# RWKV stage of a hybrid encoder: two PSUM banks for the outputs, one for x, scores of a and r in banks of their own, first retention step one round later

## The chip, the cores and the metric

The kernel runs on one core of a Trainium2 chip. The metric is the device time of one launch in microseconds: the median of three runs before the change is 3579.34 us, from 3575.51 to 3581.64.

## The reference, cut to what matters

Two layers, each with a mixer of three head groups (retention, RWKV-7, differential attention) and a feed-forward part, over 1024 positions of 1024 features in float32. The change touches the RWKV-7 group and the retention group that is recorded beside it. The recurrence that the RWKV stage computes, for six heads of 64 and two directions, is

```
def step(S, inp):
    w_t, k_t, v_t, r_t, a_t, b_t = inp
    S = (S * w_t[..., None, :]
         + jnp.einsum('dbhvk,dbhk->dbhv', S, a_t)[..., None] * b_t[..., None, :]
         + v_t[..., :, None] * k_t[..., None, :])
    return S, jnp.einsum('dbhvk,dbhk->dbhv', S, r_t)
_, ys = lax.scan(step, jnp.zeros((2, B, H, N, N), f32), seqs)
y = ys[0] + jnp.flip(ys[1], 1)
```

Retention is `scores @ V` with a decay mask inside chunks of 128, and a state per chunk that a scan carries on.

## The kernel before, in words

The scan over 1024 steps is done in chunks of 64: inside a chunk the steps are solved with a 64 by 64 triangular inverse, between chunks a state S is handed on. Two heads share the 128 partitions, so there are three head pairs; with two directions and two halves of the sequence that makes twelve units a layer, and each unit has eight chunks.

For a unit, `rwkv_prep` (L514) loads its inputs, forms decays (a scan, tile `cs`, L547) and exponentials, and then the tiles `AR` (a and r side by side), `B` and `K`. Then it multiplies `B` with `AR` on TensorE: in the kernel before, four chunks at a time, a and r together, into a PSUM tile `sbp` of one bank. VectorE masks the r half into `BP` and ScalarE copies the a half into `N` in four pieces. `rwkv_inv` inverts the 32 by 32 blocks of `N` on VectorE (tiles `NB`, `YB`, `TB`), `rwkv_merge` (L639) joins them (`z3ps`, `y3ps`, `zps`, `yps`; L674 is a transpose on VectorE), `rwkv_key` makes `SK` and `kT`, and `rwkv_prod` makes `P`.

The chain itself is `rwkv_rec` (L731), one chunk a call in four steps: `x` on TensorE, `U` (a copy of x by ScalarE), `ns` on TensorE, and `S` (ScalarE) with the output `y` (TensorE). `rwkv` (L856) runs rounds w = -2 to 11 of 16 slots each. In a round the chain handles the second half of unit w and the first half of unit w + 1, interleaved two slots apart; beside it, generators get a number of steps per round: the preparation of unit w + 4 has 13, the inverse of w + 3 has 16, key and merge of w + 2 have 6 and 12, and retention (`ret_all`) has `RSTEP` = 10. Round -2 has no chain step yet. The outputs of a round collect in one PSUM tile `y`; in slot 2 of the following round ScalarE (first half of the sequence) or VectorE (second half) reads it.

After the loop every instruction of an engine is tied to the one recorded before it, so the order on each engine inside the stage is the order of recording. Only against instructions outside the stage, the projections ahead of it, may the scheduler still shift it.

PSUM has eight banks here: two pools of two for all passing tiles (`bank`, L959, takes them in turn), and four for `x` (two), `ns` (one) and `y` (one).

Of the kernel before, what the change touches and what calls it, by code (L numbers as in the profile page):

```python
# [10 lines left out]
F32 = mybir.dt.float32  # L11
F32R = mybir.dt.float32r
AF = mybir.ActivationFunctionType
ALU = mybir.AluOpType
# [155 lines left out]
def _ori(ap, d, off, n):  # L170
    return ap[:, off:off + n] if d == 0 else _rev(ap, off, n)


def _ch(ap, t=64):
    return ap.rearrange("p (c t) -> p c t", t=t)


class Net:
# [335 lines left out]
    def rwkv_prep(self, l, st, u, d, res):  # L514

        nc, X = self.nc, self.X
        p = st["p"]
        dd = self.der[l][:, 18 + p * 8:18 + (p + 1) * 8]
        o = (u if d == 0 else 1 - u) * 512
        lo = []  # L520
        for s in range(2):
            t = X.tile([128, 512], F32, tag=f"lo{s}", name="lo")
            nc.sync.dma_start(out=t, in_=self.lod[s][:, o:o + 512])
            lo.append(t)
        ld = []
        for i, src in enumerate((self.kkd, self.xrd, self.xkd)):
            t = X.tile([128, 512], F32, tag=f"q{i}", name=("kkh", "xrh", "xkh")[i], bufs=1)
            nc.sync.dma_start(out=t, in_=src[p][:, o:o + 512])
            ld.append(t)
        yield 1  # L530
        ps = self.bank([128, 512], "wps")
        self.mm(ps, self.l2[:, d, 0], lo[0])
        yield
        lw = X.tile([128, 512], F32, tag="t1", name="lw")
        self.act(lw, ps, AF.Tanh, scale=0.5, bias=dd[:, d:d + 1])
        self.free(ps)
        ps = self.bank([128, 512], "aps")
        self.mm(ps, self.l2[:, d, 1], lo[1])
        yield
        cf = CF  # L540
        self.act(lw, lw, AF.Identity, scale=cf, bias=self.cf[:, 0:1])
        ta = X.tile([128, 512], F32, tag="t4", name="ta")
        self.act(ta, ps, AF.Tanh, scale=0.5, bias=dd[:, 2 + d:3 + d])
        self.free(ps)
        yield
        e2 = cs = X.tile([128, 512], F32, tag="t2", name="cs")
        nc.vector.tensor_tensor_scan(cs, self.c[:, K_RST:K_RST + 512], _ori(lw, d, 0, 512), 0.0,  # L547
                                     ALU.mult, ALU.add)
        e1 = self.e1
        yield  # L550
        self.act(e1[:, :, 1:65], _ch(cs), AF.Exp)
        self.act(cs, cs, AF.Exp, scale=-1.0)
        wc = X.tile([128, 8], F32, tag="WC", name="WC", bufs=5)

        kd = X.tile([128, 512], F32, tag="t1", name="kd")
        self.act(kd, ta, AF.Identity, scale=dd[:, 4:5], bias=dd[:, 5:6])
        yield
        self.act(wc, e1[:, :, 64])
        ar = X.tile([128, 8, 2, 64], F32, tag="AR", name="AR", bufs=5)

        BP = X.tile([128, 8, 128], F32, tag="BP", name="BP", bufs=3)
        B = X.tile([128, 8, 64], F32, tag="B", name="B", bufs=3)
        K = X.tile([128, 8, 64], F32, tag="K", name="K", bufs=3)
        rm = self.c[:, K_RM:K_RM + 128]
        kko = _ch(_ori(ld[0], d, 0, 512))
        xro = _ch(_ori(ld[1], d, 0, 512))
        tao = _ch(_ori(ta, d, 0, 512))
        ke = X.tile([128, 8, 64], F32, tag="t6", name="ke")
        nc.vector.scalar_tensor_tensor(out=ke, in0=kko, scalar=-0.5, in1=_ch(e2), op0=ALU.mult, op1=ALU.mult)
        q = [slice(4 * b, 4 * b + 4) for b in range(2)]  # L570
        self.tt(ar[:, q[0], 1, :], xro[:, q[0]], e1[:, q[0], 1:65], ALU.mult)

        N = X.tile([128, 8, 64], F32, tag="N", name="N", bufs=3)
        for b in range(2):
            yield
            nc.vector.scalar_tensor_tensor(out=B[:, q[b]], in0=tao[:, q[b]], scalar=1.0, in1=ke[:, q[b]],
                                           op0=ALU.add, op1=ALU.mult)
            self.tt(ar[:, q[b], 0, :], kko[:, q[b]], e1[:, q[b], 0:64], ALU.mult)
            if b == 0:
                self.tt(ar[:, q[1], 1, :], xro[:, q[1]], e1[:, q[1], 1:65], ALU.mult)  # L580
        yield 1
        for b in range(2):

            ps = self.bank([128, 4, 128], "sbp")
            for n in range(4):
                self.mm2(ps[:, n], B[:, 4 * b + n], ar[:, 4 * b + n].rearrange("p a t -> p (a t)"))
            if b == 0:
                self.tt(kd, kd, ld[2], ALU.mult)
                kv, ev = (_ch(kd), _ch(e2)) if d == 0 else (_ch(kd)[:, ::-1, :], _ch(e2)[:, :, ::-1])
            else:  # L590
                self.tt(K, kv, ev, ALU.mult)
                nc.sync.dma_start(out=self.kdd[p][d, :, o:o + 512], in_=kd)
            yield
            self.tt(BP[:, q[b], 64:128], ps[:, :, 64:128], rm[:, None, 64:128].to_broadcast([128, 4, 64]),
                    ALU.mult)
            self.act(N[0:32, q[b]], ps[0:32, :, 0:64])
            self.act(N[32:64, q[b], 0:32], ps[32:64, :, 32:64])
            self.act(N[64:96, q[b]], ps[64:96, :, 0:64])
            self.act(N[96:128, q[b], 0:32], ps[96:128, :, 32:64])
            self.free(ps)  # L600
        res.update(N=N, d=d, i=p * 4 + u * 2 + d, AR=ar, BP=BP, WC=wc, B=B, K=K)

    def rwkv_inv(self, a):
# [35 lines left out]
    def rwkv_merge(self, a):  # L639

        nc = self.nc
        N, L, NB, N3 = a["N"], self.L, a["NB"], self.N3[a["i"] % 2]

        Ld, Z, Yd = NB[:, 0:8], NB[:, 8:16], N[:, :, 0:32]
        H4 = [slice(hb * 32, hb * 32 + 32) for hb in range(4)]
        ps = self.bank([128, 8, 32], "z3ps")
        for n in range(8):
            for hb, r in enumerate(H4):
                self.mm(ps[r, n], N3[r, n], Ld[r, n], tile_position=(hb * 32, hb * 32))
        yield  # L650
        self.act(Z, ps)
        self.free(ps)
        yield 1
        ps = self.bank([128, 8, 32], "y3ps")
        for n in range(8):
            for hb, r in enumerate(H4):
                self.mm(ps[r, n], Yd[r, n], Z[r, n], stop=False, tile_position=(hb * 32, hb * 32))
            for hb, r in enumerate(H4):
                self.mm(ps[r, n], self.ident[r, r], Ld[r, n], start=False, tile_position=(hb * 32, hb * 32))
        yield  # L660
        y22, zt = N[:, :, 0:32], N[:, :, 32:64]
        for hb in (1, 3, 0, 2):
            r = H4[hb]
            self.act(L[r, :, hb % 2 * 32:hb % 2 * 32 + 32], ps[r])
        self.free(ps)
        yield 1

        ps = self.bank([128, 512], "zps")
        for n in range(8):
            for h in range(2):  # L670
                r = h * 64
                self.mm(ps[r + 32:r + 64, n * 32:(n + 1) * 32], N[r:r + 32, n, 32:64], L[r:r + 32, n, 0:32],
                        tile_position=(r, r + 32))
        nc.vector.transpose(out=y22, in_=L[:, :, 32:64])  # L674
        yield
        for r in (32, 96):
            self.act(zt[r:r + 32], ps[r:r + 32, 0:256].rearrange("p (n j) -> p n j", j=32))
        self.free(ps)
        yield 1
        ps = self.bank([128, 512], "yps")  # L680
        for n in range(8):
            for r in (32, 96):
                self.mm(ps[r:r + 32, n * 32:(n + 1) * 32], y22[r:r + 32, n, :], zt[r:r + 32, n, :],
                        tile_position=(r, r))
        yield
        for r in (32, 96):
            self.act(L[r:r + 32, :, 0:32], ps[r:r + 32, 0:256].rearrange("p (n j) -> p n j", j=32))
        self.free(ps)
# [42 lines left out]
    def rwkv_rec(self, st, u, d, s, n, y):  # L731

        nc = self.nc
# [3 lines left out]
        V = self.Vd[(2 * st["p"] + nh) % 4][:, c]  # L737
        S = st["S"][d]
        SK, AR, P = s["SK"][:, n], s["AR"][:, n], s["P"][:, n]
        x = self.psr.tile([128, 64], F32, tag="x", name="x", bufs=2)  # L740
        self.mm2(x, SK[:, 0:64], V, stop=S is None)
        if S is not None:
            self.mm2(x, AR[:, 0], S, start=False)
# [112 lines left out]
    def rwkv(self, l):  # L856
# [32 lines left out]
        ret = [self.ret_all(l), RSTEP, 0, 0]  # L889
        first = len(self.nc.cur_bb.bb.instructions)  # L890
        active, outs = [], []
        for w in range(-2, 12):
            p, j = divmod(w, 4)
            beside = []
# [10 lines left out]
            q, j2 = divmod(w + 2, 4)  # L905
# [3 lines left out]
                beside.append([self.rwkv_bonus(l, sts[p]), 12, 0, 0])  # L909
            if w > 0 and j == 0:  # L910
                beside.append([self.rwkv_fin(l, sts[p - 1]), 13, 0, 0])
            beside.append(ret)
            for g in range(16):
                n, k = divmod(g, 4)
                if g == 0 and -2 < w < 12:
                    y = self.psr.tile([128, 2, 4, 64], F32, tag="y", name="y")

                for i, m in ((w, n + 4), (w + 1, n)):
                    if 0 <= i < 12 and w > -2 and k == i % 2 * 2:
# [716 lines left out]
```

## Time and profile before

| what | value |
|---|---|
| median of three runs | 3579.34 us |
| profiled execution | 3579.7 us |
| its span, first to last instruction | 3577.9 us |
| TensorE busy | 3222.8 us, 90% of the span |
| VectorE busy | 2004.6 us, 56% |
| ScalarE busy | 1576.7 us, 44% |
| GpSimd busy | 943.7 us, 26% |
| mean granted TensorE clock | 0.946 |
| rounds -1 to 11 of layer 0 | from about 590 to 965 us |
| rounds -1 to 11 of layer 1 | from about 2358 to 2731 us |

A row of the profile names engine, line, operation, output and inputs by the program's names. PE is TensorE's matmul, PEld its weight load, DVE VectorE, ACT ScalarE, SP the queue that issues most transfers. Since `L194`, `L188` and `L185` are the lines of helpers that record every matmul, tensor-tensor operation and activation, the tile names tell the place. A number in square brackets is idle time of the engine just ahead of the row, and behind the arrow stands what ended it. A float32 matmul of the program stands in the trace as two records.

### The profile page before, as it was taken

The numbers are of one execution on the slowest core, as the hardware profiler recorded it, in microseconds if no ns is written. First come the engines' busy times: TensorE is split into PE (matmuls) and PEld (weight loads), VectorE is DVE, ScalarE is ACT, GpSimd is POOL, SyncE is SP. The second block draws the span as 40 slices with busy tenths as digits, with TensorE's granted clock in tenths as the row PEclk, the third lists the DMA queues.
The fourth block names the chain that finished last, engine by engine and source line by source line (L and its number), as shares of the span: only waits on it lengthen the run. The fifth ranks groups of instructions, "written<-read, shape, count | busy, mean of one in ns | idle before, by whom it ended". The sixth has DMA issues, their size and how long they took to land. (4 is left out here: it accounts for less than half of the span.)

```text
span 3577.9 us, 69843 instructions
## 1 busy us (share of the span) xinstructions
PE 3222.8 (90%) x28380; PEld 2601.8 (73%) x28380; DVE 2004.6 (56%) x3749; ACT 1576.7 (44%) x3071; POOL 943.7 (26%) x800
## 2 busy tenths in 40 slices
PE   6999797898787999999989997978986989999997
PEld 4777586787565888888867775867774758888886
DVE  4698425766329555552338974167662485555523
ACT  4566443666424333342236664346654342333322
POOL 3222120000026544532132221200000364554220
PEclk9999798998888999999989998989988989999998
DMA  5444334432341222283053433244325212223821
GB/s 167 154 147 123 112 106 132 145 124 72 127 146 47 86 80 83 83 285 121 26 161 123 151 117 118 96 143 139 122 83 175 83 59 80 86 83 99 278 71 47
DMA packets 214057, 418.93 MB, mean 117 GB/s; under 512 B 23876, under 2 KB 58948, under 8 KB 213700
## 3 DMA queue, kind: packets, MB, share of 16 engines
q1 hardware_dynamic: 191000, 378.53, 32.2%
q10 hardware_dynamic: 12672, 23.07, 1.7%
q0 software_dynamic: 10064, 12.85, 1.6%
q8 instruction: 224, 3.67, 0.4%
q14 instruction: 97, 0.79, 0.1%
HBM read 313.67 MB, written 100.70 MB: 116 GB/s over the span
## 5 line engine op out<-in xcount | busy, mean ns | idle before, releaser
L188 POOL TENSOR_TENSOR wll<-wr,whh 128x512 fp32r<-128x512 f32 x416 | 558.4, 1345 | 1616.8 <-ACT whh L185 1610.9
L185 ACT ACTIVATE whh<-wr 128x512 fp32r<-128x512 f32 x416 | 261.1, 631 | 625.8 <-PE sp L194 166.0
L194 PE MATMUL dps<-hl,whh 128*128 128x512 f32 x960 | 383.7, 400 | 6.6 <-DVE hl L188 3.6
L194 PE MATMUL dps<-hh,whh 128*128 128x512 f32 x960 | 387.7, 404 | 1.1 <-DVE stl L377 1.0
L194 PE MATMUL dps<-hh,wll 128*128 128x512 f32 x960 | 383.1, 399 | 0.4 <-POOL wll L188 0.4
L194 PE MATMUL sp<-hh,whh 128*128 128x512 f32 x704 | 279.2, 397 | 9.2 <-ACT hh L185 8.6
L194 PE MATMUL sp<-hl,whh 128*128 128x512 f32 x704 | 281.8, 400 | 2.1 <-POOL hl L188 1.9
L194 PE MATMUL sp<-hh,wll 128*128 128x512 f32 x704 | 276.9, 393 | 1.3 <-POOL wll L188 1.3
L194 PE MATMUL dn<-hl,whh 128*128 128x512 f32 x704 | 274.9, 391 | 0.5 <-DVE hl L188 0.5
L194 PE MATMUL dn<-hh,whh 128*128 128x512 f32 x704 | 274.1, 389 | 1.3 <-ACT hh L185 1.3
L194 PE MATMUL dn<-hh,wll 128*128 128x512 f32 x704 | 273.9, 389 | 0.0
L188 POOL TENSOR_TENSOR wll<-ws,whh 128x512 fp32r<-128x512 f32 x132 | 194.1, 1470 | 177.2 <-ACT whh L185 177.2
L188 DVE TENSOR_TENSOR hl<-hidr,hh 128x512 fp32r<-128x512 f32 x144 | 138.2, 977 | 170.4 <-ACT hh L185 161.5
L194 PEld LDWEIGHTS dps<-hl,whh 128*128 128x128 f32 x960 | 183.6, 191 | 51.8 <-POOL hl L188 6.1
L194 PE MATMUL sp<-sl,whh 128*128 128x512 f32 x528 | 211.3, 400 | 8.8 <-POOL sl L188 6.1
L194 PEld LDWEIGHTS dps<-hh,whh 128*128 128x128 f32 x960 | 183.7, 191 | 45.9 <-issue 4.4
L194 PE MATMUL sp<-sh,whh 128*128 128x512 f32 x528 | 209.8, 397 | 3.1 <-ACT as L185 3.1
L194 PEld LDWEIGHTS dps<-hh,wll 128*128 128x128 f32 x960 | 183.2, 191 | 38.8 <-issue 2.4
L194 PE MATMUL sp<-sh,wll 128*128 128x512 f32 x528 | 211.0, 400 | 0.0
L185 ACT ACTIVATE whh<-ws 128x512 fp32r<-128x512 f32 x132 | 83.5, 632 | 242.7 <-PE sp L194 138.5
L185 ACT ACTIVATE pt<-pt,mx 128x1024 f32<-128x1024 f32 x128 | 147.0, 1149 | 59.6 <-DVE mx L1216 57.3
L194 PEld LDWEIGHTS sp<-hh,whh 128*128 128x128 f32 x704 | 133.9, 190 | 41.1 <-ACT hh L185 9.4
(275 smaller groups left out, 7297.6 us busy)
## 6 DMA issues: line engine op xcount, KB each, us to landing
hidr<-hid SPq DMA_DIRECT2D x144, 256.0 KB, 4.9
bias<-t SPq DMA_DIRECT2D x64, 512.0 KB, 3.8
wr<-in_w_in_dram SPq DMA_DIRECT2D x120, 256.0 KB, 2.9
wr<-in_w_gate_dram SPq DMA_DIRECT2D x44, 512.0 KB, 3.4
wr<-in_w_up_dram SPq DMA_DIRECT2D x44, 512.0 KB, 3.3
wr<-in_w_down_dram SPq DMA_DIRECT2D x44, 512.0 KB, 4.1
pr<-st SPq DMA_DIRECT2D x56, 256.0 KB, 2.3
lo<-lod SPq DMA_DIRECT2D x48, 256.0 KB, 3.2
```

Of the source, the lines that this page charges most:

```text
L185: self.nc.scalar.activation(out=out, in_=in_, func=func, **kw)
L188: (eng or self.nc.vector).tensor_tensor(out=out, in0=a, in1=b, op=op)
L194: self.nc.tensor.matmul(out, lhsT, rhs, start=start, stop=stop, **kw)
```

## The change

Five edits. In `rwkv_prep` the scores of a and of r become two products of eight chunks each, in a bank of their own: `sap`, read by ScalarE alone, and `srp`, read by VectorE alone, one step later; `K` is formed between them. In `rwkv_merge` the transpose of L674 is recorded one step later. `x` has one PSUM buffer, `y` two. In round -2 retention gets one step, its first loads, recorded ahead of the slots, and no other.

```
-        for b in range(2):
-            ps = self.bank([128, 4, 128], "sbp")
-            for n in range(4):
-                self.mm2(ps[:, n], B[:, 4 * b + n], ar[:, 4 * b + n].rearrange("p a t -> p (a t)"))
...
-            yield
-            self.tt(BP[:, q[b], 64:128], ps[:, :, 64:128], rm[:, None, 64:128].to_broadcast([128, 4, 64]),
-                    ALU.mult)
-            self.act(N[0:32, q[b]], ps[0:32, :, 0:64])
...
+        ps = self.bank([128, 8, 64], "sap")
+        for n in range(8):
+            self.mm2(ps[:, n], B[:, n], ar[:, n, 0])
+        self.tt(kd, kd, ld[2], ALU.mult)
...
+        yield
+        self.act(N[0:32], ps[0:32])
+        self.act(N[64:96], ps[64:96])
+        self.act(N[32:64, :, 0:32], ps[32:64, :, 32:64])
+        self.act(N[96:128, :, 0:32], ps[96:128, :, 32:64])
+        self.free(ps)
+        self.tt(K, kv, ev, ALU.mult)
+        nc.sync.dma_start(out=self.kdd[p][d, :, o:o + 512], in_=kd)
+        yield 1
+        ps = self.bank([128, 8, 64], "srp")
+        for n in range(8):
+            self.mm2(ps[:, n], B[:, n], ar[:, n, 1])
+        yield
+        self.tt(BP[:, :, 64:128], ps, rm[:, None, 64:128].to_broadcast([128, 8, 64]), ALU.mult)
+        self.free(ps)
...
-        nc.vector.transpose(out=y22, in_=L[:, :, 32:64])
         yield
         for r in (32, 96):
             self.act(zt[r:r + 32], ps[r:r + 32, 0:256].rearrange("p (n j) -> p n j", j=32))
         self.free(ps)
+        nc.vector.transpose(out=y22, in_=L[:, :, 32:64])
...
-        x = self.psr.tile([128, 64], F32, tag="x", name="x", bufs=2)
+        x = self.psr.tile([128, 64], F32, tag="x", name="x", bufs=1)
...
-            beside.append(ret)
+            if w > -2:
+                beside.append(ret)
+            else:
+                next(ret[0])
...
-                    y = self.psr.tile([128, 2, 4, 64], F32, tag="y", name="y")
+                    y = self.psr.tile([128, 2, 4, 64], F32, tag="y", name="y", bufs=2)
```

VectorE at the end of the projections, before: `st` ends the projections, `rsw` and `rq` are retention's rotation, and `cs` (L547), `ke`, `AR` and `B` belong to the preparation of unit 2 in round -2.

```order
L389 SCALAR_TENSOR_TENSOR st<-st,dps 128x512 x2
L188 TENSOR_TENSOR rsw<-rsw,rope 128x1024
L188 TENSOR_TENSOR rq<-rq,rope 128x1024
L547 SCALAR_TENSOR_TENSOR cs<-c,lw 128x512
L188 TENSOR_TENSOR rq<-rq,rsw 128x1024
L569 SCALAR_TENSOR_TENSOR ke<-kkh,cs 128x512
L188 TENSOR_TENSOR AR<-xrh,e_3467 128x4x64
L188 TENSOR_TENSOR SK<-skp,c 128x512
```

The same place in the changed kernel, where `xs` is the last but one step of the projections:

```order
L407 SCALAR_TENSOR_TENSOR xs<-raw,par_74,xs 128x511
L389 SCALAR_TENSOR_TENSOR st<-st,dps 128x512 x2
L569 SCALAR_TENSOR_TENSOR ke<-kkh,cs 128x512
L188 TENSOR_TENSOR AR<-xrh,e_3467 128x4x64
L188 TENSOR_TENSOR SK<-skp,c 128x512
L576 SCALAR_TENSOR_TENSOR B<-ta,ke 128x256
L188 TENSOR_TENSOR AR<-kkh,e_3467 128x4x64
```

The three retention rows are gone from here, and so is the scan of `cs`. It now stands some thirty rows earlier, ahead of the projections' steps of the second head pair (`xs`, L405):

```order
L638 STREAM_TRANSPOSE N<-NB 128x8x32
L547 SCALAR_TENSOR_TENSOR cs<-c,lw 128x512
L405 SCALAR_TENSOR_TENSOR xs<-raw,par_74,xs 128x511
L407 SCALAR_TENSOR_TENSOR xs<-raw,par_74,xs 128x512
L405 SCALAR_TENSOR_TENSOR xs<-raw,par_74,xs 128x512
```

TensorE in round -1, layer 0, before; `pps` makes P, `sbp` is the product of B with a and r for unit 3, `sps` is retention's:

```order
L194 MATMUL x<-S,AR 64x64 x2
L194 MATMUL skp<-AR,K 64x128 x8
L194 MATMUL pps<-BP,L 64x128 x8
L194 MATMUL sbp<-AR,B 64x128 x16
L194 MATMUL ns<-Vd_4983,kT 64x64 x2
L194 MATMUL ns<-S,c 64x64 x2
```

The same place in the changed kernel:

```order
L194 MATMUL x<-S,AR 64x64 x2
L194 MATMUL sap<-AR,B 64x64 x16
L194 MATMUL skp<-AR,K 64x128 x8
L194 MATMUL pps<-BP,L 64x128 x8
L194 MATMUL ns<-Vd_5005,kT 64x64 x2
L194 MATMUL ns<-S,c 64x64 x2
L194 MATMUL ns<-U,P 64x64 x2
L194 MATMUL srp<-AR,B 64x64 x16
L194 MATMUL y<-P,U 64x64 x2
```

The two halves of `sbp`, which stood back to back, are now two products with other work between them: `sap` ahead of `skp` and `srp` behind the three products of `ns`.

## Rows read from the trace of the kernel before

**Rows 1.** Stretches of layer 0: us, busy time of PE, PEld, DVE, ACT, POOL, granted clock, DMA share, GB/s.

```profile
568.00:593.00 25.00, 10.11 (x142) 8.96 (x142) 19.51 (x26) 8.02 (x20) 0.00 (x0) 0.52 0.59 173
593.00:965.00 372.00, 329.75 (x8059) 278.82 (x8059) 231.32 (x580) 219.90 (x567) 0.75 (x8) 0.92 0.34 109
```

**Rows 2.** Timeline, layer 0, 560 to 590: start, us, instruction, idle before and releaser.

```profile
560.14 1.02 PE L194 MATMUL aps<-lo,l 128*128 128x512 f32 x2
...
561.20 0.69 ACT L185 ACTIVATE ta<-aps,der 128x512 f32<-128x512 f32 x1 [0.26 <-PE aps L194]
...
564.81 1.04 PE L194 MATMUL skp<-AR,K 64*64 64x128 f32 x16
...
572.53 1.23 DVE L188 TENSOR_TENSOR rsw<-rsw,rope 128x1024 f32<-128x1024 f32 x1 [10.88 <-DMA rsw<-pr]
...
574.81 1.22 DVE L547 TENSOR_TENSOR_SCAN cs<-c,lw 128x512 f32<-128x512 f32 x1
...
576.06 0.63 ACT L185 ACTIVATE e<-cs 128x512 f32<-128x512 f32 x1 [13.18 <-DVE cs L547]
...
577.39 0.69 DVE L569 SCALAR_TENSOR_TENSOR ke<-kkh,cs 128x512 f32<-128x512 f32 x1 [0.24 <-ACT cs L185]
...
579.83 3.68 PE L194 MATMUL sbp<-AR,B 64*64 64x128 f32 x32 [13.98 <-DVE AR L188]
...
586.57 3.68 PE L194 MATMUL pps<-BP,L 64*64 64x128 f32 x32 [3.06 <-ACT N L185]
...
590.03 0.42 PE L194 MATMUL x<-Vd,SK 64*64 64x64 f32 x4
```

**Rows 3.** Timeline of layer 1 at the same place.

```profile
2348.27 3.68 PE L194 MATMUL sbp<-AR,B 64*64 64x128 f32 x32 [13.22 <-DVE AR L188]
...
2358.60 0.42 PE L194 MATMUL x<-Vd,SK 64*64 64x64 f32 x4
```

**Rows 4.** Timeline of layer 0 inside the projections, 402 to 423.

```profile
402.21 3.68 PE L194 MATMUL sbp<-AR,B 64*64 64x128 f32 x32 [9.92 <-DVE YB L188]
...
422.26 0.69 ACT L185 ACTIVATE lw<-lw,cf 128x512 f32<-128x512 f32 x1
```

**Rows 5.** Groups by line and tile, both layers: busy, mean ns, idle before by releaser.

```profile
L194 PE MATMUL y<-P,U 64*64 64x64 f32 x768 | 61.8, 240 | 17.3 <-DVE TB L188 10.6 <-DVE y L188 5.9 <-ACT U L185 0.8
...
L185 ACT ACTIVATE N<-sbp 32x256 f32<-32x256 f32 x192 | 61.8, 322 | 64.1 <-DVE BP L188 61.0
...
L194 PE MATMUL x<-Vd,SK 64*64 64x64 f32 x768 | 58.3, 230 | 3.5 <-ACT Vd L185 3.1 <-issue 0.4
...
L194 PE MATMUL sbp<-AR,B 64*64 64x128 f32 x768 | 57.7, 301 | 58.8 <-DVE AR L188 27.2 <-DVE YB L188 19.9 <-ACT N L185 8.9
...
L185 ACT ACTIVATE U<-x 128x64 f32<-128x64 f32 x192 | 42.6, 222 | 16.3 <-PE x L194 15.0
```

**Rows 6.** Timeline of layer 0, start of round 2, 681 to 682.

```profile
681.05 0.37 ACT L185 ACTIVATE NB<-z3ps 128x256 f32<-128x256 f32 x1
...
681.66 0.48 PE L194 MATMUL y<-P,U 64*64 64x64 f32 x4 [2.75 <-DVE y L188]
```

**Rows 7.** Timeline of layer 0, round -1: two products that waited for nothing.

```profile
603.75 1.10 PE L194 MATMUL btp<-c,K 64*64 64x64 f32 x32
...
610.58 1.04 PE L194 MATMUL sbp<-AR,B 64*64 64x128 f32 x16
```

**Rows 8.** Four stretches of layer 0 at the low clock: the second, and their sum.

```profile
708.00:719.00 11.00, 7.52 (x187) 4.23 (x176) 10.57 (x22) 2.33 (x5) 0.00 (x0) 0.53 0.39 122
...
sum 32.00, PE 25.26 PEld 18.10 DVE 25.31 ACT 12.07 POOL 0.00; mean PE 6.32 PEld 4.52 DVE 6.33 ACT 3.02 POOL 0.00
```

**Rows 9.** The transpose of L674, both layers: durations in ns, then what its engine waited for.

```profile
L674 DVE STREAM_TRANSPOSE N<-L x24: 439/445/447, 417.5 to 2688.0; 128x256 f32<-128x256 f32 x24
...
  ACT L L185: 58.7, 16
```

**Rows 10.** Timeline of layer 0, round 10.

```profile
949.46 0.33 PE L194 MATMUL ns<-Vd,kT 64*64 64x64 f32 x4 [2.98 <-ACT S L185]
```

More of the change, by code (lines that the diff above doesn't have):

```diff
@@ L581, in rwkv_prep @@
         yield 1
-        for b in range(2):
-            ps = self.bank([128, 4, 128], "sbp")
-            for n in range(4):
-                self.mm2(ps[:, n], B[:, 4 * b + n], ar[:, 4 * b + n].rearrange("p a t -> p (a t)"))
[L587 to L592, printed above, removed]
-            yield
-            self.tt(BP[:, q[b], 64:128], ps[:, :, 64:128], rm[:, None, 64:128].to_broadcast([128, 4, 64]),
-                    ALU.mult)
-            self.act(N[0:32, q[b]], ps[0:32, :, 0:64])
[L597 to L600, printed above, removed]
+        ps = self.bank([128, 8, 64], "sap")
+        for n in range(8):
+            self.mm2(ps[:, n], B[:, n], ar[:, n, 0])
+        self.tt(kd, kd, ld[2], ALU.mult)
+        kv, ev = (_ch(kd), _ch(e2)) if d == 0 else (_ch(kd)[:, ::-1, :], _ch(e2)[:, :, ::-1])
+        yield
[13 more added lines that the diff above has]
+        self.free(ps)
         res.update(N=N, d=d, i=p * 4 + u * 2 + d, AR=ar, BP=BP, WC=wc, B=B, K=K)
```

## The prediction

> **What bounds the kernel now.** I read the stretches first, to see which engine is nearly full where. The rounds of the RWKV stage take 372 us in layer 0, and TensorE is busy for 329.75 of them; just ahead of them lie 25 us in which it works for 10.11 and VectorE for 19.51, at a granted clock of 0.52 [rows 1]. So inside the rounds TensorE sets the time, with some 42 us of idle; in the 25 us ahead of them it waits for others. Outside the stage no instruction is changed, and TensorE is as good as full there, so all of the change must come out of the two stages. The timeline says what the waits are, the groups by tile how much each kind sums to.
>
> The wait ahead of the rounds is a chain. TensorE ends `skp` at 565.85 and then idles 13.98 us for VectorE's `AR` [rows 2]. VectorE itself had stood 10.88 us at retention's `rsw`, whose load had not landed, and `cs` of unit 2 was queued behind it, though ScalarE had made its input `lw` at 422.95 already [rows 2, 4]. ScalarE, in turn, idled 13.18 us for `cs`. So a transfer that nobody in round -2 needs holds back the first chain step.
>
> **The change part by part.** First, the retention step a round later. By the order in the section on the change, `rsw` and `rq` leave this place and `cs` moves up to where its input is ready, in a stretch where VectorE mostly waits for projections; its 1.22 us cost nothing there. What is late next is `ta`, on ScalarE at 561.20 [rows 2]. Behind its end at 561.89 stand in order a copy of like size to `e` and the two exponentials, 0.63 us each, and some 0.4 us in which the copy waits for its product, so `ke` can start near 564.2 instead of 577.39. From `ke` to the first matmul 2.44 us went by [rows 2]; `sap` then starts near 566.6, and with a short wait for the second half of `AR` `sap` and `srp`, 1.1 us each [rows 7], end near 569.3. `N` needs some 2 us behind `sap`, to 570.2 (two copies of 512 elements, as long as `e`, and two of half that), and `pps` then takes 2.08 us for its 32 records if the clock is high: the row says 3.68 at the low clock, and 16 of its kind take 1.04 at the high one [rows 2, 7]. The first `x` starts near 572.4 instead of 590.03: 17.6 us. In layer 1 the idle is 13.22 instead of 13.98 [rows 3], so I take 16.8. Together 34.4 us. If the clock stays low here, about 1.6 us a layer less for `pps`.
>
> The moved work is not gone. In a round VectorE has about eight of these operations of 1.22 us to do later, 9.8 us a layer. With VectorE busy 231 of 372 us [rows 1] most of it lies beside TensorE's work, but the first round has it in one piece: I charge 2 us a layer, 4 in all, and keep 9.8 a layer as the bound. The new order also moves retention's later loads behind the loads of unit 3 on SP's queue, and puts its first ones where they were; unit 3's loads wait for none of it longer than before. At the end retention has its last steps one round later, in rounds 10 and 11, where TensorE waits for the chain anyway (2.98 us behind one `S` [rows 10]). There its table loads and exponentials delay the chain as they did in round 10; I take nothing, between 4 us of gain and 4 of loss a layer.
>
> Second, `sap` and `srp`. The price on TensorE is 2 x 1.10 against 2 x 1.04 us [rows 7]: 0.12 us for each of 24 units, 2.9 us. ScalarE saves: four copies instead of eight, near 2 us instead of 8 x 0.322 = 2.6 [rows 5], and its 61.0 us of waiting for `BP` [rows 5] fall away, since the two readers no longer share a bank. Most of that idle costs nothing by itself. What it costs TensorE is the 8.9 us in which the second `sbp` waits for `N` to free its bank [rows 5]; that I take whole. Inside the projections `sbp` of unit 1 waits 9.92 us behind VectorE's chain for unit 0 [rows 4], 19.9 us in both layers [rows 5]. That chain starts with `N`, which comes some 2 to 3 us earlier when it need not wait for `BP`; I take 2.5 a layer, 5 in all, between 0 and 8.
>
> Here a rule speaks against the edit. The product of 32 records with 64 columns took 1.10 us, 34 ns a record, against 65 ns for each of the 16 of 128 columns [rows 7]. The Trainium skill, "TensorE: Matmul & The Clock Gate", section "Wait — 56ns, not 53.3ns?", states that with hardware decode off the sequencer spends about 62 ns on every matmul, which binds when a matmul is shorter than that. By that, as an estimate, `sap` and `srp` would take 64 x 62 ns = 4.0 us instead of 2.08, 1.9 us more a unit and 45 us in all. The trace does not agree: 34 ns is below that floor.
>
> Third, `y` in two banks. `y` waited 16.5 us for VectorE (10.6 put down to `TB`, the row just behind the reader of `y`, and 5.9 to `y`) [rows 5]. At 681.66 the wait was 2.75 us, but the product after it needs `NB`, which ScalarE finishes at 681.42 [rows 6]: there only about 1 us is gained. I take two thirds of the sum, 11 us; the bounds are 4 and 16.5.
>
> Fourth, the clock. Behind the longer waits the granted clock falls to its lower level, 1.2 GHz. Four such stretches in layer 0, which follow waits that this change removes, sum to 32 us with 25.26 us of TensorE work at half speed [rows 8]; at full speed that would be 12.6 less. Other waits stay, and in the worst stretch ones for `U` and `Vd` are among the causes, so I take a third, 4 us a layer and 8 in all, between 0 and 25.
>
> Fifth, what can cost. The late transpose: 24 of 0.445 us [rows 9], now issued one step before `yps` needs them instead of two; behind other VectorE work each could be waited for. Against that, VectorE no longer stands 58.7 us for `L` in front of them [rows 9]. I charge 6 us; the bounds are 10.7 of loss and 10 of gain. One bank for `x`: a new `x` now waits for the last `U`. In almost every slot the `ns` of the other direction stands ahead of it on TensorE (visible in the order as `ns<-U,P` before the next `x`) and needs the same `U`, so the wait is there already; only the last chunk of a unit pair has no `ns`. I charge 2 us; the bound is a rival below.
>
> The sum: 34.4 + 8.9 + 5 + 11 + 8 = 67.3 gained, 4 + 2.9 + 6 + 2 = 14.9 lost, 52.4 us in all. Against the profiled execution's 3579.7 us that is 3527 us; that execution lies 0.4 us above the median of the runs, so nothing is to be moved.
>
> **The rivals.** *Paid back in the rounds.* The stall ahead of the rounds goes, but VectorE, with 9.8 us of retention more in the early rounds and a late transpose, makes TensorE wait again, and the clock stays as it is. For it: in the stretch 708 to 719 VectorE is busy 10.57 of 11 us with the rotation while TensorE works 7.52 [rows 8], and that rotation comes at another point of every head pair now. Then the 11 and the 8 us go and the 4 become 19.6 - 4 = 15.6 more at most, half of which I count: 52.4 - 19 - 8 = 25, so 3554 us.
>
> *Everything given back.* All of 16.5 us of `y` and 25 us of the clock are saved and the transposes cost nothing: 52.4 + 5.5 + 17 + 6 = 81, so 3499 us. For it: VectorE is idle 140 us a layer; against: waits for `S` and `U` stay.
>
> *One bank for x serialises the directions.* If every `x` had to wait for a `U` that TensorE does not need otherwise, the price would be x and U end to end, 0.230 + 0.222 us [rows 5], for 192 steps 87 us: 3527 + 87 = 3614 us. It makes the kernel slower from 52.4 / 192 = 0.27 us a step on. Against it is the order, in which `ns` comes first.
>
> *A floor on every matmul.* Were a record of 64 columns to cost as much as one of 128, 65 ns, the two products would take 4.2 us instead of 2.2, 2 us for each of 24 units: 3527 + 48 = 3575 us. It is the mechanism of the Trainium skill's page above. Against it are the 34 ns of `btp`.
>
> **How the numbers follow.** The forecast has 0.62, paid back 0.18, everything given back 0.13, serialised 0.04, the floor 0.01, and 0.02 is left for what I do not see. Its own range is 3510 to 3545. The range of 8 in 10 reaches to both neighbours, 3497 to 3557, which are also about the sums at the bounds of `y`, the clock and the transpose. About 7 us, 0.2%, is what a measurement of this kernel can tell from no change. Forecast, paid back, everything and part of the rest are faster by more than that: 0.93; the floor and half of what I do not see lie within it: 0.03; the rest is slower: 0.04.
>
> **What would show it.** In the profile after, VectorE's `rsw` should come behind the first chain step, the idle before `sap` of unit 2 should be near 1 us instead of 14, and from the end of the projections to the first `x` there should be 12 us instead of 30. `N` should wait for `sap` and not for `BP`. `y` should wait for `U` alone. Right, but with the second case: waits of `yps` for `N` by L674's successor, or of `skp` and `vtp` for `SK`. Wrong would be the whole argument if the first `x` came no earlier, or if `x` waited for `U` in most of its 192 steps.

## The result, and the profile after

The changed kernel takes 3537.27 us (median of four runs, 3533.37 to 3540.1), the kernel before beside it 3577.43 us. The ratio is 0.9886, 95% interval 0.9869 to 0.9903: 40.2 us less, where 52.4 were forecast. The profiled execution has a span of 3537.3 us.

The timeline of layer 0 at the same place as in [rows 2], after the change (start, us, engine, line, instruction, idle before and releaser):

```profile
558.35 1.02 PE L194 MATMUL aps<-lo,l 128*128 128x512 f32 x2
...
559.40 0.69 ACT L185 ACTIVATE ta<-aps,der 128x512 f32<-128x512 f32 x1 [0.26 <-PE aps L194]
...
560.98 0.62 ACT L185 ACTIVATE e<-cs 128x512 f32<-128x512 f32 x1
...
562.30 0.69 DVE L569 SCALAR_TENSOR_TENSOR ke<-kkh,cs 128x512 f32<-128x512 f32 x1 [2.44 <-ACT cs L185]
...
564.74 0.68 PE L194 MATMUL sap<-AR,B 64*64 64x64 f32 x16 [0.68 <-DVE AR L188]
...
566.17 1.10 PE L194 MATMUL srp<-AR,B 64*64 64x64 f32 x32
...
566.38 1.96 ACT L185 ACTIVATE N<-sap 32x512 f32<-32x512 f32 x4 [2.83 <-PE sap L194]
...
568.40 1.96 PE L194 MATMUL pps<-BP,L 64*64 64x128 f32 x32 [1.13 <-ACT N L185]
...
570.19 0.28 PE L194 MATMUL x<-Vd,SK 64*64 64x64 f32 x4
```

From `aps` to the first `x` it is 11.84 us, where it was 29.89. `e` waits for nothing, `sap` waits 0.68 us instead of 13.98, and the retention's `rsw` starts only at 572.23, behind the first chain step. In layer 1 `sap` waits 0.69 us instead of 13.22 [rows 3], and from `aps` to `x` it is 11.85 us, where it was 29.26.

The rounds, from the first `U` of a layer to its last, of the kernel before (us, busy time of PE, PEld, DVE, ACT, POOL, granted clock, DMA share, GB/s; layer 0, then layer 1):

```profile
591.10:961.30 370.20, 329.41 (x8080) 278.76 (x8071) 232.69 (x582) 218.24 (x568) 0.75 (x8) 0.92 0.34 108
2359.60:2729.30 369.70, 329.50 (x8085) 277.80 (x8076) 232.84 (x582) 218.67 (x568) 0.75 (x8) 0.92 0.34 108
```

And of the changed one:

```profile
571.20:938.80 367.60, 325.83 (x8341) 276.74 (x8340) 240.03 (x577) 210.88 (x532) 0.74 (x8) 0.93 0.36 116
2319.50:2686.10 366.60, 325.58 (x8340) 276.06 (x8340) 240.06 (x577) 211.01 (x531) 0.74 (x8) 0.93 0.36 116
```

The rounds are 5.7 us shorter in two layers. TensorE's busy time falls by 7.5 us although it has more records; its idle time, span less busy, is 82.8 us after 81.0. So in this trace nearly all of the gain lies ahead of the rounds, and the waits that the prediction took away in the rounds have others in their place. The groups show which (both layers, columns as in [rows 5]):

```profile
L194 PE MATMUL y<-P,U 64*64 64x64 f32 x768 | 61.2, 238 | 0.8 <-ACT U L185 0.8
...
L194 PE MATMUL x<-Vd,SK 64*64 64x64 f32 x768 | 56.9, 226 | 0.2
...
L185 ACT ACTIVATE N<-sap 32x512 f32<-32x512 f32 (+1 forms) x96 | 46.1, 480 | 24.8 <-PE sap L194 23.9
...
L194 PE MATMUL y3ps<-NB,N 32*32 32x32 f32 x1536 | 36.1, 210 | 20.9 <-ACT NB L185 16.9 <-issue 4.0
...
L194 PE MATMUL srp<-AR,B 64*64 64x64 f32 x768 | 29.1, 230 | 4.1 <-ACT N L185 4.1
L194 PE MATMUL sap<-AR,B 64*64 64x64 f32 x768 | 28.9, 227 | 21.6 <-DVE YB L188 16.3 <-DVE B L576 2.6 <-DVE AR L188 1.8
```

`y` has lost its 16.5 us of waits for VectorE, `N` its 61.0 us behind `BP`, and `x` waits for nothing. New are 16.9 us of `y3ps` behind ScalarE's `NB`, and `z3ps` waits 19.9 us where it waited 12.1. The transpose, recorded later, waits no more (0.7 us where it was 58.7 [rows 9]), and nothing waits for it:

```profile
L680 DVE STREAM_TRANSPOSE N<-L x24: 409/438/446, 415.9 to 2640.3; 128x256 f32<-128x256 f32 x24
...
  ACT L L185: 0.7, 2
```

Where the wait of `y` went is read from the timeline at the start of round 4, layer 0:

```profile
714.13 0.20 ACT L185 ACTIVATE U<-x 128x64 f32<-128x64 f32 x1
...
718.77 1.22 DVE L188 TENSOR_TENSOR rQ<-rq,rc 64x1024 f32<-64x1024 f32 x1
...
720.02 0.42 DVE L188 TENSOR_TENSOR y<-y,yT 128x256 f32<-128x256 f32 x1
...
720.48 0.38 ACT L185 ACTIVATE yT<-y 128x256 f32<-128x256 f32 x1 [6.15 <-DVE y L188]
...
720.76 0.38 ACT L185 ACTIVATE NB<-z3ps 128x256 f32<-128x256 f32 x1
...
721.19 0.33 PE L194 MATMUL y3ps<-NB,N 32*32 32x32 f32 x8 [2.66 <-ACT NB L185]
```

VectorE's `y` is late behind the rotation and, from 716.0 to 718.3, two transposes of the inverses. TensorE's `y` no longer cares, having another bank. But here, where a head pair ends, ScalarE's `yT` overwrites columns that VectorE's `y` still reads, so ScalarE stands 6.15 us. `NB<-z3ps` is queued behind it, and TensorE waits for that. The wait has moved one step on.

### The profile page after: what moved, and what is told of

Same layout as the page of the kernel before. It is cut to its first block, busy times and chain, and to the rows that moved or that the text cites. A ratio compares the mean times of both kernels' runs of the same rounds, so it can differ in the third digit from the quotient of the medians.

```text
span 3537.3 us, 71264 instructions
## 1 busy us (share of the span) xinstructions
PE 3213.3 (91%) x29148; PEld 2595.5 (73%) x29148; DVE 2002.5 (57%) x3725; ACT 1555.9 (44%) x2975; POOL 941.8 (27%) x800
## 4 chain that ended last, share of the span: by engine, by line
PE 72%; DVE 11%; DMA 6%; ACT 5%; issue 2%; POOL 2%; SPq 0%; DVEq 0%; ACTq 0%; POOLq 0%
PE sp L194 22%; PE dn L194 13%; PE dps L194 13%; PE aps L194 4%; DMA wr<-in_w_in_dram 2%; PE ns L194 2%; PE y L194 2%; DVE pt L1217 1%; PE pv L194 1%; PE tps L1247 1%; POOL wll L188 1%; ACT L185 1%; DVE x L188 1%; PE s L194 1%; PE yps L194 1%
## 5 line engine op out<-in xcount | busy, mean ns | idle before, releaser
L194 PEld LDWEIGHTS dps<-hl,whh 128*128 128x128 f32 x960 | 183.0, 191 | 52.4 <-POOL hl L188 6.1
```

The source lines that it names most:

```text
L194: self.nc.tensor.matmul(out, lhsT, rhs, start=start, stop=stop, **kw)
```

## The experiments

The theory at first (A in the expectations) was what the trace seems to say: the retention edit is nearly all of the gain, the rest next to nothing. The rival (B) is that the other edits gain in the rounds, and the moved retention work takes it back there. The runs are told by subject. Each was compared with runs of the kernel before on the same chip. The times are medians and the ratios are to the kernel before; differences in us are worked out from the ratios where the text does not name the medians, and the difference of two of these ratios is uncertain by 8 to 10 us. Rows and waits come from one profiled execution of each kernel.

**The retention edit alone.**

```diff
-            beside.append(ret)
+            if w > -2:
+                beside.append(ret)
+            else:
+                next(ret[0])
```

> The kernel before with one edit of the change: the first retention step is taken a round later. Theory A (the gain is the head's): between aps and the first x of the stage the trace of after shows 18.05 us less per layer, and the rounds next to nothing more, so this edit alone saves 33 to 37 us: 3541 to 3545 us. Rival B (the new banks gain some 25 us in the rounds, and the moved retention work takes half of the head's 36 us back out of the same rounds): this edit alone saves about 20 us, 3555 to 3560 us.

3565.28 us, ratio 0.9959 (0.9943 to 0.9974): 14.7 us less, far from A and short even of B. The head had gained all that was forecast, 17.7 and 17.1 us from `aps` to `x`, but the rounds took 379.6 and 382.2 us, 21.9 us more than before (this profiled execution is 6.5 us above its median):

```profile
572.00:951.60 379.60, 329.46 (x8052) 275.70 (x8051) 240.84 (x590) 217.43 (x568) 0.74 (x8) 0.93 0.35 112
2336.50:2718.70 382.20, 327.87 (x8052) 276.05 (x8052) 241.12 (x590) 217.52 (x567) 0.74 (x8) 0.94 0.34 111
```

The timeline in round 3 shows one part of the price:

```profile
715.10 1.22 DVE L188 TENSOR_TENSOR rsw<-rsw,rope 128x1024 f32<-128x1024 f32 x1 [2.06 <-DMA rsw<-pr]
...
716.24 1.22 DVE L188 TENSOR_TENSOR rq<-rq,rope 128x1024 f32<-128x1024 f32 x1
...
717.65 0.42 DVE L188 TENSOR_TENSOR BP<-sbp,c 128x256 f32<-128x256 f32 x1
...
718.10 1.32 ACT L185 ACTIVATE N<-sbp 32x256 f32<-32x256 f32 x4 [4.34 <-DVE BP L188]
...
719.47 0.91 PE L194 MATMUL sbp<-AR,B 64*64 64x128 f32 x6 [3.99 <-ACT N L185]
```

VectorE waits for a load of the retention and rotates; `BP` comes late, ScalarE's `N` reads the same bank behind `BP`, and TensorE's next `sbp` wants that bank. Over both layers `sbp` waits 18.1 us for `N`, twice the 8.9 of [rows 5]. That is 9 us of the 22; among the others `x<-S,AR` waits 9.1 us for ScalarE's `S` (0.1 before) and `vtp` 8.6 us for VectorE's `SK` (4.0 before).

**The other edits without it**, the inverse of that diff on the changed kernel.

> The changed kernel without the retention edit (scores, banks and transpose as changed, the first retention step in its old place). Theory A: what is left is the 3.3 us in the projections of the two layers and the rounds' 5.7 us less what these rounds gain from other places, so 3 to 9 us under the kernel before: 3568 to 3574 us. Rival B: the banks keep their 25 us, 3550 to 3556 us.

3558.27 us, 0.9935 (0.992 to 0.9951): 23.3 us less. A falls: the other edits are worth more than the retention edit. Their rounds take 363.0 and 363.6 us, and `sap` in the head still waits 13.49 us. Yet even so the head, `aps` to `x`, is 4.6 us shorter than before in layer 0 and 4.3 in layer 1; layer 0:

```profile
561.42 1.02 PE L194 MATMUL aps<-lo,l 128*128 128x512 f32 x2
...
586.68 0.28 PE L194 MATMUL x<-Vd,SK 64*64 64x64 f32 x4
```

The two parts sum to 38.0 us of the 40.2 measured, but in the profiled executions this hides two departures that cancel. The heads gain 34.8 us by the retention edit alone and 8.9 by the others alone, and 35.5 together. The rounds grow by 21.9 us with the one and shrink by 13.3 with the others, and shrink by 5.7 with both. So about 8 us of the head are gained by either, and the others take away most of what the moved retention costs. What is left is theory C of the later expectations: each edit gains, and waits taken away come back in part one step on.

**Without the scores' own banks.**

```diff
-        ps = self.bank([128, 8, 64], "sap")
...
-        ps = self.bank([128, 8, 64], "srp")
...
+        for b in range(2):
+            ps = self.bank([128, 4, 128], "sbp")
...
```

> The changed kernel with the scores of a and r in one bank again, four at a time (sbp), the rest as changed. If the scores' own banks are worth what the prediction put on them (8.9 us of waits for ScalarE's N, 5 us in the projections, less 2.9 us for 64-column matmuls), it is 11 us slower than after: about 3548 us. Theory A: only what the trace of after shows in the projections, 3.3 us, and at most 2 us in the rounds: 3539 to 3543 us.

3560.93 us, 0.9949 (0.9933 to 0.9965): about 22 us slower than the changed kernel. Both expectations were too small. `sbp` waits 20.6 us for `N` here, and the rounds take 377.6 and 374.2 us.

**One bank for y, two for x again.**

```diff
-        x = self.psr.tile([128, 64], F32, tag="x", name="x", bufs=1)
+        x = self.psr.tile([128, 64], F32, tag="x", name="x", bufs=2)
...
-                    y = self.psr.tile([128, 2, 4, 64], F32, tag="y", name="y", bufs=2)
+                    y = self.psr.tile([128, 2, 4, 64], F32, tag="y", name="y")
```

> The changed kernel with one bank for the outputs and two for x again. By the prediction (y in two banks 11 us, one bank of x -2 us) it is 9 us slower than after: 3546 us, with the wait of PE's y for VectorE's y back at some 16 us in the list of groups. Theory A (the wait went one step on, to ScalarE's yT behind VectorE's read, and so to y3ps): 0 to 4 us slower, 3537 to 3541 us, the 16 us of waits back on y but gone from y3ps, z3ps and ns.

3545.1 us, 0.9905 (0.9888 to 0.9921): 7 us slower than the changed kernel, which the uncertainty doesn't part from 0 nor from the 9 forecast. The groups show the exchange:

```profile
L194 PE MATMUL y<-P,U 64*64 64x64 f32 x768 | 61.5, 239 | 21.9 <-ACT yT L185 20.6 <-ACT U L185 0.8 <-DVE y L188 0.5
...
L194 PE MATMUL y3ps<-NB,N 32*32 32x32 f32 x1536 | 35.4, 208 | 6.5 <-issue 5.5 <-ACT NB L185 1.0
```

With one bank 20.6 us stand at `y`, with two 16.9 stand at `y3ps`.

**The two banks alone**, the opposite edit on the kernel before.

> The kernel before with the banks alone: two for y, one for x. By the prediction 16.5 us of waits at y go, of which 11 count, less 2 for x: 3569 us. By the theory that the wait goes on to ScalarE's yT, behind VectorE's y, and from there to y3ps: 3574 to 3578 us, with 10 us or more of new waits at y3ps and z3ps.

3572.28 us, 0.9976 (0.9964 to 0.9989): 8.6 us less, as the prediction's terms say (11 less 2). In this company the wait goes on to `y3ps` only in part: `y` waits 0.8 us, and `y3ps` 5.1 us for `NB`. The rounds of both layers:

```profile
590.20:955.80 365.60, 322.72 (x8084) 273.49 (x8073) 232.45 (x582) 218.07 (x567) 0.75 (x8) 0.95 0.34 109
2358.00:2723.90 365.90, 327.76 (x8084) 277.70 (x8072) 232.52 (x582) 218.40 (x567) 0.75 (x8) 0.93 0.34 109
```

They are 8.4 us shorter than before, and all of that is TensorE's busy time: its idle time there is 81.0 us, as before. So the 16.5 us of `y` have others in their place (`ns` for `S` 25.8 us instead of 22.9, for one), and what fell is the time that the same matmuls take, at a granted clock of 0.95 and 0.93 instead of 0.92.

**ScalarE's copy first where a head pair ends.**

```diff
+ self.yX = X.tile([128, 256], F32, name="yX")
...
-        o = _ori(self.yT, d, nh * 512, 512)[:, sl]
+        o = (_ori(self.yX, d, 0, 256) if (st["p"], nh, d) == (1, 0, half) else _ori(self.yT, d, nh * 512, 512)[:, sl])
...
-                    for o in outs:
+                    for o in sorted(outs, key=lambda o: o[0] % 4 // 2):
```

> The changed kernel; where a pair of heads ends (rounds 3 and 7 of each layer) ScalarE's copy of the next pair's first outputs is taken ahead of VectorE's sum of the last ones, and goes to 256 columns of its own, so that it overwrites nothing that the sum still reads. Theory C (the 16 us of waits of PE's y on one bank live on behind ScalarE's yT, which waits for VectorE's y, and come back at y3ps and z3ps): the 15.9 us at y3ps and most of the 5.3 us at z3ps go, ScalarE's gap of some 6 us before yT goes, and the time falls by 8 to 16 us to 3521 to 3529 us. Rival D (these waits lie beside others that end as late: VectorE is late anyway, and B, SK or TB is waited for instead): 0 to 4 us, 3533 to 3538 us.

3533.38 us, 0.987 (0.985 to 0.9891). The mechanism is as C says:

```profile
713.84 0.36 ACT L185 ACTIVATE yX<-y 128x256 f32<-128x256 f32 x1
714.31 0.38 ACT L185 ACTIVATE NB<-z3ps 128x256 f32<-128x256 f32 x1
720.11 1.15 ACT L185 ACTIVATE fq<-y 128x512 f32<-128x512 f32 x2 [5.42 <-DVE y L188]
```

`NB` is there 6 us sooner, and `y3ps` waits 1.0 us for it in all. But ScalarE now stands 5.42 us at the next reader of VectorE's `y`, with `S` of the chain behind it, and `ns` waits for `S` 22.3 us instead of 18.5. The median falls by 4 us, which the intervals don't part from none; C's 8 us are not reached by it, but not excluded either. By the medians a quarter of some 16 us of waits taken away was on the path.

**The transpose in its old place.**

```diff
+        nc.vector.transpose(out=y22, in_=L[:, :, 32:64])
         yield
...
         self.free(ps)
-        nc.vector.transpose(out=y22, in_=L[:, :, 32:64])
```

> The changed kernel with VectorE's transpose of L in its old place, ahead of ScalarE's zt. The prediction charged the late place with 6 us: 3531 us. By the trace of after no instruction waits for that transpose, and VectorE would wait here again for ScalarE's L (58.7 us before): 3537 to 3545 us.

3548.01 us, 0.9913 (0.9894 to 0.9931): about 10 us slower than the changed kernel. Its VectorE stands 71.8 us for `L` at 19 transposes, as here in round 2:

```profile
667.89 0.45 DVE L676 STREAM_TRANSPOSE N<-L 128x256 f32<-128x256 f32 x1 [5.62 <-ACT L L185]
...
668.56 1.22 DVE L547 TENSOR_TENSOR_SCAN cs<-c,lw 128x512 f32<-128x512 f32 x1
```

Behind it is queued `cs`, from which the next unit's scores come. But this isn't shown to be the way to TensorE: `sap` waits no longer than in the changed kernel (21.7 us against 21.6). What grew there is `vtp` behind VectorE's `SK`, 9.0 us against 4.2, and `y3ps` behind `NB`, 20.2 against 16.9.

**The transpose moved alone**, on the kernel before.

> The kernel before with the transpose alone moved: VectorE takes it behind ScalarE's zt instead of ahead of them. By the prediction's charge (the late place costs 6 us) it is 3584 us. If VectorE's wait of 58.7 us for ScalarE's L held up the VectorE work queued behind it, as the changed kernel with the early transpose suggests (10 us slower than after), it is 5 to 12 us faster than before: 3566 to 3573 us.

3565.12 us, 0.9963 (0.9948 to 0.9979): 13.2 us less from one line moved. The prediction had charged 6. VectorE stands 14.7 us for `L` there instead of 58.7. The rounds of both layers:

```profile
589.30:949.10 359.80, 321.85 (x8080) 272.26 (x8070) 232.79 (x582) 218.11 (x567) 0.75 (x8) 0.94 0.35 111
2347.90:2714.60 366.70, 326.15 (x8080) 276.46 (x8068) 233.08 (x582) 218.35 (x568) 0.75 (x8) 0.93 0.35 109
```

They are 13.4 us shorter than before; 10.9 of these are TensorE's busy time and 2.5 its idle time.

**The retention at 11 steps a round.**

```diff
-RSTEP = 10
+RSTEP = 11
```

> The changed kernel with the retention's pace raised from 10 to 11 steps a round, so that it ends about as early as before although it begins a round later. Theory C (part of the head's gain is given back at the end: the last 8 steps of the chain take 11.4 us against 4.7, and the last gps comes 2.1 us later per layer, since the retention's last steps now fall in the last round): the last two rounds are back at 23 us from 27, 8 to 12 us faster in two layers, 3526 to 3530 us. Rival E (the retention work costs the same wherever it falls): within 3 us of after, 3534 to 3540 us.

3539.82 us, 0.9886 (0.9866 to 0.9906): no gain. The last two rounds are as C says, 20.90 us; first the changed kernel, then this one (rounds -1 to 9, and 10 with 11):

```profile
571.20:911.90 340.70, 303.87 (x7915) 258.30 (x7916) 234.79 (x568) 197.15 (x498) 0.74 (x8) 0.92 0.38 120
911.90:938.80 26.90, 21.96 (x434) 18.44 (x428) 5.24 (x9) 13.73 (x35) 0.00 (x0) 0.93 0.18 64
```

```profile
575.30:926.50 351.20, 307.58 (x7994) 261.59 (x7996) 235.24 (x570) 199.35 (x500) 0.75 (x8) 0.95 0.36 118
926.50:947.40 20.90, 17.17 (x354) 14.28 (x348) 3.86 (x7) 12.60 (x33) 0.00 (x0) 0.84 0.23 79
```

In layer 0 the end gains 6.0 us and the rounds ahead of it lose 10.5; in layer 1, from the same steps of the chain, it is 6.0 and 4.6. The whole is the same, as rival E has it: in this schedule a faster pace only shifts the price of the retention's work. Why the rounds ahead grow is not shown.

**N in halves again**, in the new banks.

```diff
-        self.act(N[0:32], ps[0:32])
+        for b in q:
+            self.act(N[0:32, b], ps[0:32, b])
...
```

> The changed kernel with ScalarE's copies of the scores, N, each cut in two halves again (192 a core, as before), the banks as changed. If the scores' gain (19 us within the stage, by the run with the old scores) is ScalarE's lighter load (15.7 us less of N), then ScalarE gets 15.7 us heavier and the time rises by 8 to 16 us: 3545 to 3553 us. If it is the banks (r's matmuls no longer wait for the copy of a), it rises by 0 to 4 us: 3537 to 3541 us.

3550.57 us, 0.9919 (0.9898 to 0.9941): about 12 us slower than the changed kernel, uncertain by about 10, so ScalarE's longer copying is a part of the scores' gain, by these values near a half. `srp` waits for `N` 8.9 us instead of 4.1.

**The last normalisation's loads early**, with ScalarE's copy first.

```diff
+        if p == 2:
+            for v, src, name in ((gl, self.lod[2], "gl"), (bo, self.bod[p], "bo")):
+                t = self.XB.tile([128, T], F32, tag="ra", name=name, bufs=5)
+                nc.sync.dma_start(out=t, in_=src)
+                v += [t[:, 0:512], t[:, 512:1024]]
```

> The kernel of the run with ScalarE's copy first, and in the last normalisation of a layer gl and bo are loaded ahead of it, into buffers that the retention has done with. The trace of after shows PE waiting 5.47 us for gl there, once a layer. If nothing else is late, that is 8 to 11 us less in two layers than the run with ScalarE's copy first: 3522 to 3526 us. Rival: VectorE's sums and products with bo, or the retention's last stores ahead on SP's queue, end as late, and it is 0 to 4 us: 3529 to 3534 us.

3530.58 us, 0.9858 (0.9841 to 0.9875). The wait for `gl` is gone: in the changed kernel, then here,

```profile
951.53 2.07 PE L194 MATMUL gps<-gl,lg 128*128 128x512 f32 x2 [5.47 <-DMA gl<-lod]
```

```profile
943.96 1.88 PE L194 MATMUL gps<-gl,lg 128*128 128x512 f32 x4
```

but the median fell by 3 us, not by 8 to 11: the rival's range.

**And two copies to GpSimd.**

```diff
-        self.act(lw, lw, AF.Identity, scale=cf, bias=self.cf[:, 0:1])
+            nc.gpsimd.tensor_scalar(out=lw, in0=lw, scalar1=cf, scalar2=cf, op0=ALU.mult, op1=ALU.add)
...
+            nc.gpsimd.tensor_scalar(out=kd, in0=ta, scalar1=dd[:, 4:5], scalar2=dd[:, 5:6],
```

> The same, and two of ScalarE's copies from SBUF to SBUF per unit (lw<-lw,cf and kd<-ta) go to GpSimd, which does next to nothing in the rounds, in 10 of the 12 units of a layer: 15.2 us of ScalarE less per layer (0.72 and 0.80 us each). If ScalarE's load is what the scores' fewer copies paid by (12 us for 15.7 us in two layers), this takes 15 to 24 us more off: 3500 to 3510 us. Rival: GpSimd's longer tensor_scalar (1.81 us at kk against 0.80 on ScalarE) delays the scan behind lw, or the two engines hold up VectorE, and it is between nothing and 8 us slower than the run without it: 3524 to 3535 us.

3528.02 us (3526.74 to 3530.51), 0.9855 (0.9839 to 0.9871): ScalarE is 12 us a layer less busy in the rounds, and that gains nothing that can be told. That speaks against ScalarE's load as such as what the scores' shorter copies paid by; `N` stands where TensorE waits for it (`srp` above). It is not proved, for VectorE is about 2 us a layer busier here (242.2 and 242.4 us in the rounds, 240.3 and 240.1 without the two copies on GpSimd), so a gain can have been paid back there. This and the version above are the fastest here, by medians 7 to 9 us under the changed kernel; their intervals still overlap its own at the edge.

## Why the prediction was right or wrong

The sign and the range were right, the sum 12 us too large, and the parts stand otherwise than forecast. That the sum came into the range is in part luck: terms that were 10 to 16 us too low offset what was counted twice or paid back.

*Head, 34.4 us.* Right in mechanism and size: 18.05 us in layer 0 against 17.6, and 17.4 in layer 1 against 16.8. But it isn't the retention edit's alone. The other edits without it already take 8.9 us off the two heads: there `N` no longer waits for `BP` (6.54 us at 585.19 in layer 0 before, with retention's rows ahead of `BP` on VectorE), and `pps` takes 2.13 us instead of 3.68.

*Moved VectorE work, 4 us.* Mis-sized low, by "most of it lies beside TensorE's work". Alone the edit gains 34.8 us in the heads and the rounds grow by 21.9; 14.7 are left by the ratios. In the changed kernel it is worth 17.5 (0.9935 less 0.9886): against the run without it the heads are 26.5 us shorter, the rounds 7.6 longer, and what follows the last `U` of layer 1 takes 851.2 us instead of 847.6. So the price there is some 11 us, above the 4 and inside the bound of 9.8 a layer. The prediction held such a price, the first rival's, for likely only together with the loss of the `y` and clock terms; the price came, and the time fell into the forecast's range all the same. One way it is paid is shown, through the bank that `BP` and `N` shared. In the changed kernel that way is gone. There TensorE's idle time in the rounds is 82.8 us with the edit and 75.9 without, and the waits that grew are `y3ps` for `NB` (16.9 us, 9.0 without), `z3ps` for `NB` (16.7, 11.6) and `ns` for `U` (7.1, 0.5). Which of these set the time is not tested, and the pace of the retention only shifts the price.

*Scores, 8.9 + 5 - 2.9 = 11 us.* Mis-sized low: some 22 us in the changed kernel. The prediction took the wait of `sbp` for `N` at the 8.9 us that it had before. With the retention in the rounds it is 20.6 (the run with the old scores), and the new banks take that away too. Without the moved retention there is little room for them: the scores, the banks of `y` and `x` and the transpose together gain 23.3 us, and the run with these banks alone has 8.6, the run with the transpose alone 13.2. Of the 5 us in the projections the trace shows 3.6 us fewer waits (`sap` 16.3 behind `YB`, `sbp` 19.9). About half of the gain hangs on the shorter copies, which the prediction put at 0.6 us a unit off TensorE's path. The 34 ns a record held: 32 records of `srp` take 1.10 us. The Trainium skill ("TensorE: Matmul & The Clock Gate", "Wait — 56ns, not 53.3ns?") puts some 62 ns on every matmul with hardware decode off; by that they would take 2.0 us, as an estimate, and the trace does not agree.

*y in two banks, 11 us, and one bank for x, -2.* Right in size: 8.6 alone, 7 +- 8 in the changed kernel, but not by the mechanism, so the size is in part luck. `y` does wait for `U` alone, 0.8 us; but its wait was handed on and not removed. In the changed kernel 16.9 us stand at `y3ps`, and in the run with the two banks alone TensorE's idle time in the rounds did not fall at all; its busy time did, by 8.4 us. `x` costs nothing by the trace, 0.2 us of waits.

*Late transpose, -6 us.* Wrong sign: 13.2 us gained alone, more than the bound of 10, and about 10 in company. The prediction weighed who waits for the transpose, and nobody does. Within the stage the edit moves nothing but this row in VectorE's order, so the gain can only come by what is queued behind it: 58.7 us of VectorE standing, which it had named as "against that" and held to be slack. By which of the rows behind it TensorE gains is not shown.

*Clock, 8 us.* The granted clock of the rounds went from 0.92 to 0.93, and TensorE's busy time there fell by 7.5 us, about as forecast. But this is no term beside the others: the runs with the two banks alone and the transpose alone have the matmuls of the kernel before, and nearly all that each gains in the rounds is TensorE's busy time (8.4 of 8.4 us, 10.9 of 13.4). What the prediction priced as fewer waits came there as the same work at a higher granted clock. This is read from one execution of each, whose two layers differ by some 5 us. In the changed kernel it is otherwise: with the transpose in its old place TensorE's idle time in the rounds is 8.0 us longer, and its busy time the same.

By these values the retention was put 13 us too high (34.4 - 4 against 17.5), some 8 of them because the head's gain is had by either part; the transpose was put 16 and the scores 11 too low. That the sum was nevertheless 12 too high suggests that the parts don't add: taken out of the changed kernel one by one they are worth 17.5, 22, 7 and 10, together 56 us where all are worth 40. For the heads the traces show it (34.8 and 8.9 us alone, 35.5 together). For the rest, that they remove in part the same waits is a reason that fits; within the uncertainty of four such differences it is not proved. The scores alone weren't run.

## What to carry to other kernels

When work is moved out of a stall, price it in the place where it lands by what is queued behind it on an engine that keeps its order, and not by that engine's share of idle time. Even on an engine that is idle a third of the time a wait need not be free: one transposition recorded a step later was worth 13 us, though nothing waited for its result. Two readers of one bank coupled their engines here: a late VectorE reached TensorE through ScalarE (4.34 us, then 3.99). An extra buffer removes a wait only if the late reader's next dependant can do without it too. And before a removed wait is counted as gain, compare the bound engine's idle and busy time over the whole stretch: with the two banks alone the waits came back elsewhere, and the gain stood in the busy time.

## What the runs showed of the hardware

In the last version GpSimd's `tensor_scalar` of 128x512 float32 for `kd` took 0.76 to 0.80 us in 16 of 20 instructions, near ScalarE's 0.80, and 1.40 to 1.57 us in the other four. Each of the four began while VectorE was in a tensor-tensor operation with both inputs in SBUF (`rq<-rq,rsw`, `rt<-rt,rg`). Two of the 16 began during one with an input in PSUM (`tps`) and were not longer:

```profile
608.06 1.26 DVE L188 TENSOR_TENSOR rkz<-tps,c 128x512 f32<-128x512 f32 x2
608.32 0.77 POOL L561 TENSOR_SCALAR kd<-ta,der 128x512 f32<-128x512 f32 x1 [5.98 <-DVE cs L551]
...
829.28 1.27 DVE L188 TENSOR_TENSOR rt<-rt,rg 128x512 f32<-128x512 f32 x2
829.53 1.57 POOL L561 TENSOR_SCALAR kd<-ta,der 128x512 f32<-128x512 f32 x1 [7.68 <-ACT L L185]
```

It also goes the other way: VectorE's `TB` at 759.64, begun 0.14 us behind such an instruction of GpSimd, took 0.52 us, where its neighbours took 0.20. So in these rows the two engines held each other up. GpSimd's `kk` in the projections took 1.55 to 2.09 us (12 instructions); whether for the same reason is not tested.
